# Five blocks of an expert table turned by the vector engine instead of TensorE, in a Trainium2 decoder layer

## The chip, the cores and the metric

The kernel runs on one core of one Trainium2 chip. The core has a matrix engine (TensorE, PE in the profile, with its weight loads as PEld), a vector engine (DVE), a scalar engine (ACT), GpSimd (POOL), a sync engine that only issues transfers (SP), and 16 DMA engines between DRAM and the on-chip memory, which all queues share. The metric is the device time of one execution in microseconds. Before the change it is 943.9 us, the median of three runs from 941.56 to 944.66 us.

## The reference: what is computed

A decoder layer over 256 tokens of width 1024, in float32. A mixer (retention beside block-sparse attention, gated, with an output projection) ends in a residual add. Then, in `peer`, each token takes part in a product-key retrieval of single-neuron experts:

```python
u = u_tab[ec]                                        # rows of peer_u, 16384 x 1024
a = jax.nn.gelu(jnp.einsum('td,thkd->thk', hc, u), approximate=False)
return jnp.einsum('thk,thkd->td', gc * a, v_tab[ec]) # rows of peer_v, 16384 x 1024
```

Each of 8 heads picks 16 experts of 16384 for a token. `ec` holds their numbers and `gc` the softmaxed gates.

## The kernel before, in words

The kernel has three stages on PE's time axis. From 0 to about 302 us it computes the mixer and the queries from weights that stream in. In the second stage, 302 to 649 us, for 176 of the 256 tokens it doesn't gather experts but multiplies with the whole table: `peer_u` is cut into 128 chunks of 128 experts, and for each chunk `c` eight matmuls (L1288) contract the 1024 columns against the transposed activations. The result passes GELU and is multiplied with a dense matrix of gates, `W`, which is built meanwhile from one-hot products (L1160 and L1161 on DVE, L1215 and L1216 on PE). In the third stage, 649 us to the end, the 128 chunks of `peer_v` are multiplied with `W` (L1320, L1321): a chunk V0, V1, ... of v is split into a rounded high part on ACT (L147) and a remainder on DVE (L148), and every tenth pair of chunks is used unsplit (L1318). The tokens that remain have their rows of u and v gathered by GpSimd (L1037) and reduced on DVE (L1048 for u, L1123 for v), woven into the same two stages.

A matmul contracts over partitions, so a chunk of u, loaded with one expert per partition, has to be turned first. Three kinds of chunk differ in who turns them.

- A plain chunk is loaded by one DMA of 512 KB in rows of 4 KB (L682), turned by eight PE transposes into two PSUM banks (L737), and copied out by two ACT instructions (L738) to a tile `rhi`. This is done two iterations ahead of its matmuls, and the matmuls use the activations in the layout `hTf`.
- Every seventh chunk up to number 125 was turned during the mixer: four DMAs of 128 KB, each with 32 partitions and 1 KB runs, brought its quarters to their places (`load_quarters`, L747), DVE turned 32x32 blocks (`turn`, L751), and the result went to a DRAM scratch, `turned`. In the second stage it is loaded from there (L705) and used in place. Its matmuls use the layout `hTd`.
- A chunk listed in the tuple `TURN` is loaded by `load_quarters` on SP's queue and turned by `turn` in the second stage. Before the change the tuple is empty, so there is none.

What sets the order: the instructions of each engine run in the order in which the program writes them. Loads of u and v go through a ring of six slots of 512 KB (`raw_ring`), in order, on SP's queue; a load waits for its slot, which is free when the PE transposes (plain chunk), the DVE turn (chunk of `TURN`), the matmuls themselves (every seventh chunk), or the DVE remainder (a chunk of v) have read it. Each load also takes one of eight completion semaphores in turn and waits for the load that had that semaphore before. The gathers go on GpSimd's own queue, paced by the loop over chunks.

Of the kernel before, what the change touches and what calls it, by code (L numbers as in the profile page):

```python
# [53 lines left out]
STEP = 7  # L54
PRE0 = 14
PERIOD = 3
TURN = ()
WARM = 8
GROW = 96
SK = 16  # L60
# [15 lines left out]
def layer_kernel(ctx, tc, x, mix_norm_g, w_in, ret_w_branch, moba_q_gain, moba_k_gain, moba_w_branch,  # L76
# [26 lines left out]
    def raw_tile(n=1):  # L103

        i = raw_count[0] % RAWS
        raw_count[0] += n
        assert i + n <= RAWS
        return raw_ring[:, i] if n == 1 else raw_ring[:, i:i + n]
# [580 lines left out]
    def load_any(i):  # L689
# [9 lines left out]
        elif i < len(pieces) + NK:  # L699
# [3 lines left out]
            if early_chunk(c):  # L703
                u_raw[c] = raw_tile()
                nc.sync.dma_start(u_raw[c], turned[c // STEP])  # L705
            elif c in TURN:
                u_raw[c] = raw_tile()
# [14 lines left out]
    def transpose_u(c):  # L722

        if c < NK and early_chunk(c):
            u_T[c] = u_raw.pop(c)
        elif c in TURN:
            r = u_raw.pop(c)
# [12 lines left out]
    def early_chunk(c):  # L740
        return c % STEP == STEP - 1 and c // STEP < NPRE
# [530 lines left out]
    for c in range(NK):  # L1272
# [11 lines left out]
        uT = u_T.pop(c)  # L1284
        hT = hTd if c in TURN or early_chunk(c) else hTf
        for k in range(KC):
# [154 lines left out]
```

## Time and profile before

| | |
|---|---|
| median of three runs | 943.9 us (941.56 to 944.66) |
| the profiled execution | 942.91 us, span on the core 941.1 us |
| PE busy | 932.6 us, 99% |
| DVE busy | 794.2 us, 84% |
| ACT busy | 521.1 us, 55% |
| POOL busy | 395.0 us, 42% |
| moved by DMA | 322.50 MB, mean 343 GB/s |

All times inside the execution are microseconds from the start of the span. The median of the runs is 1.0 us above the profiled execution, and that lies 1.8 us above its own span. PE, PEld, DVE, ACT and POOL are told apart by the busy time of each. [...] q1 is the queue of loads that SP issues, q0 that of GpSimd's gathers and q10 ACT's.

### The profile page before, as it was taken

The numbers are of one execution on the slowest core, as the hardware profiler recorded it, in microseconds if no ns is written. First come the engines' busy times: TensorE is split into PE (matmuls) and PEld (weight loads), VectorE is DVE, ScalarE is ACT, GpSimd is POOL, SyncE is SP. The second block draws the span as 40 slices with busy tenths as digits, with TensorE's granted clock in tenths as the row PEclk, the third lists the DMA queues.
The fourth block names the chain that finished last, engine by engine and source line by source line (L and its number), as shares of the span: only waits on it lengthen the run. The fifth ranks groups of instructions, "written<-read, shape, count | busy, mean of one in ns | idle before, by whom it ended". The sixth has DMA issues, their size and how long they took to land.

```text
span 941.1 us, 19115 instructions
## 1 busy us (share of the span) xinstructions
PE 932.6 (99%) x7192; PEld 894.4 (95%) x7192; DVE 794.2 (84%) x1518; ACT 521.1 (55%) x953; POOL 395.0 (42%) x305
## 2 busy tenths in 40 slices
PE   8999999999999999999999999999999999999998
PEld 6887898998999999999999999999999999999997
DVE  6658557788678999999998999974979989898977
ACT  6554655544644435444687778776454645454553
POOL 3412010000202447534656667763547556464720
PEclk9999999999999999999999999999999999999999
DMA  9899879998799997999999999999999999999993
GB/s 317 236 236 283 241 207 292 306 295 264 244 354 386 406 400 285 402 402 361 375 401 390 382 364 381 380 377 367 370 363 398 409 383 409 383 409 374 409 344 125
DMA packets 110858, 322.50 MB, mean 343 GB/s; under 512 B 11532, under 2 KB 23701, under 8 KB 110638
## 3 DMA queue, kind: packets, MB, share of 16 engines
q1 hardware_dynamic: 64492, 184.43, 55.0%
q0 software_dynamic: 32512, 115.54, 32.5%
q10 hardware_dynamic: 13762, 21.31, 7.6%
q8 instruction: 57, 0.93, 0.4%
q14 instruction: 35, 0.29, 0.1%
HBM read 308.57 MB, written 14.19 MB: 343 GB/s over the span
## 4 chain that ended last, share of the span: by engine, by line
PE 95%; DMA 2%; DVE 1%; ACT 0%; POOL 0%; issue 0%; SPq 0%; DVEq 0%; ACTq 0%; POOLq 0%
PE acc L1288 24%; PE side L737 11%; PE side L1320 9%; PE acc L1320 9%; PE acc L230 6%; PE acc L231 6%; PE acc L232 6%; PE acc L1321 4%; PE side L1321 4%; PE acc L239 3%; PE acc L240 3%; PE acc L241 3%; DMA raw_ring<-in_peer_v_dram 2%; PE side L1318 1%; PE acc L1318 1%; PE acc L1216 1%
## 5 line engine op out<-in xcount | busy, mean ns | idle before, releaser
L1037 POOL DMA_INDIRECT rows<-in_peer_u_dram,eg x86 | 110.5, 1285 | 68.4 <-DVE rows L1048 30.2
L1037 POOL DMA_INDIRECT rows<-in_peer_v_dram,eg x54 | 96.0, 1777 | 73.2 <-DVE vacc L1123 51.2
L737 PE MATMUL side<-ident,raw_ring 128*128 128x128 f32 x768 | 103.0, 277 | 0.0
L737 PEld LDWEIGHTS side<-ident,raw_ring 128*128 128x128 f32 x768 | 93.0, 192 | 0.0
L1165 ACT ACTIVATE oh_buf<-oh_more,tS 128x128 bf16<-128x128 f16 x176 | 58.4, 417 | 0.5 <-DVE oh_more L1160 0.5
L1123 DVE SCALAR_TENSOR_TENSOR vacc<-rows,av,vacc 128x1024 f32<-128x1024 f32 x43 | 55.1, 1282 | 0.1
L1048 DVE SCALAR_TENSOR_TENSOR rows<-rows,h 128x1024 f32<-128x1024 f32 x43 | 53.2, 1249 | 1.4 <-DMA rows<-in_peer_u_dram,eg 1.4
L1260 ACT ACTIVATE cw<-W 128x352 fp32r<-128x352 f32 x58 | 28.7, 495 | 45.3 <-PE acc L1321 43.9
L1261 DVE TENSOR_TENSOR cw<-W,cw 128x352 fp32r<-128x352 f32 x58 | 30.2, 521 | 19.8 <-ACT cw L1260 19.6
L1246 POOL TENSOR_TENSOR W<-W,gl 128x256 f32<-128x256 f32 (+19 forms) x31 | 26.4, 850 | 41.9 <-ACT gl L1245 34.0
L580 POOL DMA_DIRECT2D x1d<-xt x1 | 0.7, 657 | 88.5 <-DVE xt L562 88.5
L1288 PE MATMUL acc<-hTd,raw_ring 128*128 128x128 f32 x288 | 35.1, 276 | 0.0
L1160 DVE TENSOR_TENSOR oh_more<-iota,tI 128x1024 f16<-128x1024 f16 x44 | 34.3, 780 | 0.0
L1161 DVE TENSOR_TENSOR oh_buf<-oh_more,tM 128x1024 f16<-128x1024 f16 x44 | 32.3, 734 | 2.2
L1288 PEld LDWEIGHTS acc<-hTd,raw_ring 128*128 128x128 f32 x288 | 33.6, 192 | 0.0
L154 POOL TENSOR_TENSOR gny<-va,minus_half 128x8 f32<-128x8 f32 x2 | 4.3, 2126 | 67.8 <-DVE va L454 67.8
L1215 PE MATMUL acc<-oh_buf 128*128 128x128 bf16 x176 | 24.4, 220 | 0.0
L1216 PE MATMUL acc<-oh_buf 128*128 128x128 bf16 x176 | 24.4, 219 | 0.0
L1229 ACT ACTIVATE W<-acc 128x512 f32<-128x512 f32 (+20 forms) x44 | 17.2, 391 | 12.0 <-PE acc L1216 10.6
L1248 ACT ACTIVATE W<-acc 128x256 f32<-128x256 f32 (+19 forms) x52 | 18.5, 356 | 4.4 <-PE acc L1288 4.4
L1231 DVE TENSOR_TENSOR W<-acc,W 128x264 f32<-128x264 f32 (+19 forms) x32 | 16.2, 507 | 4.7 <-ACT W L1229 4.5
L1215 PEld LDWEIGHTS <-oh_buf 128*128 128x128 f16 x176 | 19.8, 114 | 0.0
(2695 smaller groups left out, 3484.4 us busy)
## 6 DMA issues: line engine op xcount, KB each, us to landing
raw_ring<-in_peer_v_dram SPq DMA_DIRECT2D x128, 512.0 KB, 8.2
raw_ring<-in_peer_u_dram SPq DMA_DIRECT2D x96, 512.0 KB, 9.9
raw_ring<-in_w_in_dram SPq DMA_DIRECT2D x52, 512.0 KB, 5.5
raw_ring<-turned SPq DMA_DIRECT2D x18, 512.0 KB, 7.1
raw_ring<-in_peer_w_q_dram SPq DMA_DIRECT2D x16, 512.0 KB, 6.1
W<-in_peer_u_dram SPq DMA_DIRECT2D x14, 512.0 KB, 11.0
eraw<-in_peer_u_dram ACTq DMA_DIRECT2D x36, 128.0 KB, 6.5
h<-in_peer_u_dram ACTq DMA_DIRECT2D x36, 128.0 KB, 6.6
```

The lines of the kernel that those rows point to most:

```text
L230: T.matmul(o[t], xh[:, s], wh, start=(k == 0), stop=False)
L231: T.matmul(o[t], xh[:, s], wl, start=False, stop=False)
L232: T.matmul(o[t], xl[:, s], wh, start=False, stop=(k == kc - 1))
L737: T.transpose(p[:, k * P:(k + 1) * P], r.rearrange("p (i k) -> p k i", k=KC)[:, 4 * q + k], ident)
L1037: G.indirect_dma_start(out=r, out_offset=None, in_=tab, in_offset=bass.IndirectOffsetOnAxis(ap=eg[:, j:j + 1], axis=0))
L1048: V.scalar_tensor_tensor(r, r, 1.0, h, op0=OP.mult, op1=OP.mult, accum_out=av[:, j:j + 1])
L1123: V.scalar_tensor_tensor(a, r, av[:, j:j + 1], a, op0=OP.mult, op1=OP.add)
L1165: A.activation(o1[:, j], hot[:, 0, :, j], AF.Copy, scale=tS[:, t, k + j:k + j + 1])
L1215: T.matmul(p[:, j * P:(j + 1) * P], hi, o1, start=True, stop=False)
L1288: T.matmul(pa[:, n:n + NA], uT[:, k * P:(k + 1) * P], hT[:, k], start=(c % 2 == 0 and k == 0), stop=(k == KC - 1), skip_group_check=True)
L1320: T.matmul(o[b][:, :2 * ND], vh[:, n], w, start=(c == 0), stop=False, skip_group_check=True)
L1321: T.matmul(o[b][:, :ND], vl[:, n], w[:, :ND], start=False, stop=(c == NK - 1), skip_group_check=True)
```

## The change

The tuple `TURN` names five chunks; nothing else is edited.

```diff
--- before.py
+++ after.py
@@ -54,7 +54,7 @@
 STEP = 7
 PRE0 = 14
 PERIOD = 3
-TURN = ()
+TURN = (122, 123, 124, 126, 127)
 WARM = 8
 GROW = 96
 SK = 16
```

Chunk 125 is one of those turned during the mixer, so from 122 on no chunk is left to PE. The code that now runs for the five chunks was there before:

```python
def load_quarters(queue, dst, c):                                  # L744
    src = peer_u[0, c * P:(c + 1) * P, :].rearrange("(b a) (g d) -> g a b d", a=32, g=4)
    for g in range(4):
        queue.dma_start(dst[32 * g:32 * g + 32].rearrange("a (b d) -> a b d", b=4), src[g])

def turn(dst, src, k):                                             # L749
    V.transpose(dst.rearrange("p (k b a) -> p b k a", k=KC, b=4)[:, :, k],
                src.rearrange("p (b k i) -> p b k i", b=4, k=KC)[:, :, k])

elif c in TURN:                                                    # in transpose_u, L726
    r = u_raw.pop(c)
    u_T[c] = hi_tile(F32)
    for k in range(0, KC, 4):
        turn(u_T[c], r, slice(k, k + 4))
```

Three places show what moves. First PE, at the end of the second stage, after its last one-hot products. The rows are the matmuls of the chunks up to 127 (`x8` is a chunk) and the first of the third stage (L1320). Before:

```order
L737 MATMUL side<-ident,raw_ring 128x128 x8
L1288 MATMUL acc<-hTf,rhi__7278 128x128 x8
L1288 MATMUL acc<-hTf,rhi__7313 128x128 x8
L737 MATMUL side<-ident,raw_ring 128x128 x8
L1288 MATMUL acc<-hTf,rhi__7347 128x128 x8
L737 MATMUL side<-ident,raw_ring 128x128 x8
L1288 MATMUL acc<-hTd,raw_ring 128x128 x8
L1288 MATMUL acc<-hTf,rhi__7382 128x128 x8
L1288 MATMUL acc<-hTf,rhi__7409 128x128 x8
L1320 MATMUL side<-cw,rhi__7433 128x352
```

Now, from chunk 122 (`rhi__7287`) to 127 (`rhi__7384`), chunk 125 being the one that is read from `raw_ring`:

```order
L1288 MATMUL acc<-hTd,rhi__7287 128x128 x8
L1288 MATMUL acc<-hTd,rhi__7315 128x128 x8
L1288 MATMUL acc<-hTd,rhi__7342 128x128 x8
L1288 MATMUL acc<-hTd,raw_ring 128x128 x8
L1288 MATMUL acc<-hTd,rhi__7367 128x128 x8
L1288 MATMUL acc<-hTd,rhi__7384 128x128 x8
L1320 MATMUL side<-cw,rhi__7398 128x352
```

The three groups of transposes here are gone, as are two more ahead of them, and the matmuls of six chunks stand one behind the other. Second DVE at the same place, where the last row products of the gathers (L1048) and the first work on v (L1261, L148) stand:

```order
 L1048 SCALAR_TENSOR_TENSOR rows__7077,av<-rows__7077,h_75 128x1024
+L751 STREAM_TRANSPOSE rhi__7287<-raw_ring 128x4x4x32 x2
 L1048 SCALAR_TENSOR_TENSOR rows__7118,av<-rows__7118,h_75 128x1024
 L1048 SCALAR_TENSOR_TENSOR rows,av<-rows,h_75 128x1024 x2
 L1109 TENSOR_TENSOR av<-av,gg 128x64
```

```order
L751 STREAM_TRANSPOSE rhi__7315<-raw_ring 128x4x4x32 x2
L751 STREAM_TRANSPOSE rhi__7342<-raw_ring 128x4x4x32 x2
L751 STREAM_TRANSPOSE rhi__7367<-raw_ring 128x4x4x32 x2
L751 STREAM_TRANSPOSE rhi__7384<-raw_ring 128x4x4x32 x2
L1261 TENSOR_TENSOR cw<-W,cw 128x2x176
```

The second piece follows the first directly. The turn of chunk 122 stands ahead of the last three row products, the other four behind them and ahead of the first work on v. Third SP's queue, the loads around the border of u and v, each with what it waits for: a `DMAHW` is one of the eight completion semaphores, PE, DVE the engine that frees the slot. Now, from chunk 125 (L705) over 126 and 127 to V0, V1 and V2:

```order
L705 DMA raw_ring_71<-turned_88 128x1024 [waits DMAHW7_49]
L747 DMA raw_ring_71<-in_peer_u_dram 32x4x256 [waits DMAHW0_49]
L747 DMA raw_ring_71<-in_peer_u_dram 32x4x256 [waits DMAHW1_49]
L747 DMA raw_ring_71<-in_peer_u_dram 32x4x256 [waits DMAHW2_49]
L747 DMA raw_ring_71<-in_peer_u_dram 32x4x256 [waits DMAHW3_49]
L747 DMA raw_ring_71<-in_peer_u_dram 32x4x256 [waits DMAHW4_49,PE_49]
L747 DMA raw_ring_71<-in_peer_u_dram 32x4x256 [waits DMAHW5_49]
L747 DMA raw_ring_71<-in_peer_u_dram 32x4x256 [waits DMAHW6_49]
L747 DMA raw_ring_71<-in_peer_u_dram 32x4x256 [waits DMAHW7_49]
L682 DMA raw_ring_71<-in_peer_v_dram 128x1024 [waits DMAHW0_49,DVE_49]
L682 DMA raw_ring_71<-in_peer_v_dram 128x1024 [waits DMAHW1_49,DVE_49]
L682 DMA raw_ring_71<-in_peer_v_dram 128x1024 [waits DMAHW2_49,DVE_49]
```

Before, this stretch was one load of `turned`, two of u and then those of v. A load that needed one place in the row of eight semaphores now needs four, so the last quarter of chunk 127 waits for the landing of chunk 125, and V0 for that of the first quarter of chunk 126.

## The prediction

> **What bounds the kernel now.** I read the page's busy shares, then the chain of waits, then the windows around the border between u and v, where all five chunks lie. First the page's row of busy times:
>
> ```profile
> PE 932.6 (99%) x7192; PEld 894.4 (95%) x7192; DVE 794.2 (84%) x1518; ACT 521.1 (55%) x953; POOL 395.0 (42%) x305
> ```
>
> PE is the bound on the whole, so work taken from it counts, as long as what it then needs is there in time. The windows show whether the DMA engines could deliver earlier (columns: window, its length, busy time of PE, PEld, DVE, ACT, POOL, granted clock, DMA share, GB/s):
>
> ```profile
> 626.00:630.00 4.00, 4.00 (x45) 4.00 (x45) 3.90 (x7) 3.50 (x10) 3.55 (x3) 1.00 0.90 330
> 630.00:634.00 4.00, 4.00 (x38) 4.00 (x38) 2.28 (x5) 2.95 (x7) 2.11 (x4) 1.00 0.95 315
> 634.00:644.00 10.00, 10.00 (x95) 10.00 (x95) 0.00 (x0) 4.06 (x10) 3.30 (x4) 1.00 1.02 409
> 645.00:647.30 2.30, 2.30 (x23) 2.30 (x23) 1.60 (x2) 1.90 (x3) 1.19 (x1) 1.00 0.33 93
> ```
>
> They are a second bound, just under the first: 0.90 to 1.02 busy until the first chunks of v have landed, and only then, from 645 to 647.3, nearly idle. So the question is not what PE saves, but whether V0 and V1 can be there that much sooner.
>
> **What is removed.** The chain of waits gives each chunk's eight transposes with the time that they hold PE (start, length, what):
>
> ```profile
> 629.82 0.95 PE side L737 x8
> ...
> 632.55 0.89 PE side L737 x8
> ...
> 635.67 0.95 PE side L737 x8
> 636.62 3.57 PE acc L1288 x32
> 640.20 0.89 PE side L737 x8
> ...
> 642.87 0.89 PE side L737 x8
> ```
>
> These are chunks 122, 123, 124, 126 and 127: 0.95 + 0.89 + 0.95 + 0.89 + 0.89 = 4.57 us of PE's path, the most that the change can give. The ten ACT copies (L738) leave too; they are off the path.
>
> **What is added on DVE.** The turn's price stands in the mixer's rows, its place in the timeline (start, length, engine, line, operation):
>
> ```profile
> L751 DVE STREAM_TRANSPOSE eT<-eraw x18: 697/705/712, 61.8 to 222.3; 128x512 f32<-128x512 f32 x18
> ...
> 631.87 0.09 DVE L1048 DVE_READ_ACCUMULATOR rows<-rows,h 128x1 f32 x1
> 632.28 0.34 DVE L1109 TENSOR_TENSOR av<-av,gg 128x64 f32<-128x64 f32 x1 [0.32 <-ACT av L1108]
> 644.85 0.53 DVE L1261 TENSOR_TENSOR cw<-W,cw 128x352 fp32r<-128x352 f32 x1 [12.23 <-ACT cw L1260]
> 645.79 1.23 DVE L148 TENSOR_TENSOR rlo__7434<-raw_ring,rhi__7433 128x1024 fp32r<-128x1024 f32 x1 [0.42 <-ACT rhi__7433 L147]
> 647.52 1.23 DVE L148 TENSOR_TENSOR rlo__7451<-raw_ring,rhi__7450 128x1024 fp32r<-128x1024 f32 x1 [0.51 <-ACT rhi__7450 L147]
> ```
>
> Two halves of 0.705 are 1.41 us a chunk, 7.05 in all. Four of the five turns, 5.64 us, fall into the 12.23 us in which DVE now waits; that hole is their cover, and without it they would stand before the first work on v. The turn of 122 pushes the last three row products back, so L1109 ends at 632.62 + 1.41 = 634.0 and the turn of 123 at 635.4. PE without its transposes wants 123 at 636.62 - 0.95 - 0.89 - 0.95 + 1.79 = 635.6 (3.57 for two chunks is 1.79 each). That fits with 0.2 us to spare, so DVE costs nothing by itself, unless data come late.
>
> **What is moved: V0 and V1.** PE begins V0 and V1 here, ACT's splits of both stand below, and the load of V0, issued at 630.80, has the time to landing at the end of its row:
>
> ```profile
> 648.87 0.41 PE L1320 MATMUL side<-cw,rhi__7433 128*128 128x352 f32 x1
> 651.10 0.36 PE L1320 MATMUL side<-cw,rhi__7450 128*128 128x352 f32 x1
> ```
>
> ```profile
> 644.70 1.06 ACT L147 ACTIVATE rhi__7433<-raw_ring 128x1024 fp32r<-128x1024 f32 x1
> 646.43 1.06 ACT L147 ACTIVATE rhi__7450<-raw_ring 128x1024 fp32r<-128x1024 f32 x1 [0.40 <-DMA raw_ring<-in_peer_v_dram]
> ```
>
> ```profile
> 630.80 18.31 SPq L682 DMA_DIRECT2D raw_ring<-in_peer_v_dram  x8
> raw_ring<-in_peer_v_dram SPq DMA_DIRECT2D x1, 512.0 KB, 13.1
> ```
>
> V0 lands at 630.80 + 13.1 = 643.9; with 1.06 of ACT and 1.23 of DVE behind that it could be ready at 646.2, 2.6 us before PE takes it. V1 lands at 646.4 (ACT waited for it), is ready at 647.52 + 1.23 = 648.75, and PE takes it at 651.10: 2.35 us of slack. So 2.35 of the 4.57 us can be had at most while the loads land as now. They can hardly land sooner: V0's slot, held by chunk 122, comes free with DVE's turn at about 629.8 instead of 630.8, but 13.1 us of waiting is a queue of transfers, and the same bytes stand ahead.
>
> **What the 1 KB runs cost.** No load in 1 KB runs stands beside gathers of 4 KB rows in this trace. The nearest rows are the mixer's, where the runs go beside the weights' 2 KB rows (121 to 122 and 197.5 to 202.5) or alone (122 to 123, every packet under 2 KB):
>
> ```profile
> 121.00:122.00 1.00, 1.00 (x11) 1.00 (x10) 0.29 (x1) 0.20 (x1) 0.00 (x0) 1.00 1.06 380
> 122.00:123.00 1.00, 1.00 (x12) 1.00 (x10) 0.00 (x0) 0.86 (x1) 0.00 (x0) 1.00 1.14 217
> 197.50:198.50 1.00, 1.00 (x6) 0.84 (x5) 0.35 (x1) 0.62 (x1) 0.00 (x0) 1.00 1.12 355
> 198.50:202.50 4.00, 4.00 (x20) 3.30 (x19) 2.73 (x3) 1.06 (x1) 0.00 (x0) 1.00 1.08 230
> ...
> DMA packets 241, 0.22 MB, mean 217 GB/s; under 512 B 29, under 2 KB 241, under 8 KB 241
> ```
>
> The engines are fully busy in all four and move as little as half of the 409 GB/s of 4 KB rows. A chunk is 0.524 MB: 1.28 us at 409, 1.38 at 380, 2.42 at 217. Over the five us from 197.5 the mean is (355 + 4 x 230)/5 = 255 GB/s, a loss of 5 x (1 - 255/409) = 1.9 us. So a chunk costs 0.1 to 1.9 us of all engines' time more than now; I take 1.13, the lone runs' row, which lies between the ends.
>
> [...]
>
> Five chunks cost 5 x 1.13 = 5.65 us. Of this the gaps take something: 626 to 634 lacks 4 x (79 + 94)/409 = 1.7 us of full rate, or by busy share 0.6 us; I take 1.2. That leaves 4.45 us by which the queue empties later (0 to 8.9 from the ends).
>
> One thing works the other way. While 1 KB runs and other packets share the engines, they take turns packet by packet (145 to 146 us, packets and MB of the two queues):
>
> ```profile
> q1 hardware_dynamic: 93, 0.19, 70.4%
> q10 hardware_dynamic: 84, 0.08, 43.8%
> ```
>
> So gathers of 4 KB rows would go ahead, V0 to V2 would come out last and alone, and V1 would land up to one load, 1.28 us, ahead of the queue's end, where it now lands with it. I take half, 0.6.
>
> **What is late next.** SP's queue holds twenty quarters instead of five loads, and the last quarter of 127 waits for the landing of chunk 125:
>
> ```profile
> 626.61 1.30 SPq L705 DMA_DIRECT2D raw_ring<-turned  x1
> DMA to landing us min/median/max: 8.4/8.4/8.4
> ...
> DMA to landing us min/median/max: 2.6/6.6/11.2
> ```
>
> The first two are chunk 125, which lands at 635.0, the last the mixer's quarters. 635.0 plus 6.6 and a turn of 1.41 is 643.0. PE, 4.57 us ahead, would end 127 at 648.87 - 4.57 = 644.3 and so wants it at 644.3 - 1.79 = 642.5. With three chunks' loss ahead (3 x 1.13 - 1.2 = 2.2) PE stands 2.7 us there, and V0 is behind 127 in SP's queue. This is less than what V1 asks for, so it doesn't add.
>
> **Sum.** V1 is ready 4.45 - 0.6 later, of which 2.35 is slack: the third stage runs 1.5 us later than now. It passes this on, since PE has no idle time there to catch up with (1.07 us in 680 to 700, none else up to 920):
>
> ```profile
> 680.00:700.00 20.00, 18.93 (x138) 18.51 (x137) 15.29 (x17) 9.99 (x12) 7.99 (x5) 1.00 0.95 345
> 700.00:720.00 20.00, 20.00 (x149) 20.00 (x148) 19.96 (x20) 9.53 (x11) 16.81 (x8) 1.00 1.00 389
> 720.00:920.00 200.00, 200.00 (x1454) 199.85 (x1452) 181.07 (x180) 104.00 (x125) 107.55 (x58) 1.00 1.01 391
> ```
>
> The profiled execution took 942.91 us and would take 944.4; the median of the runs is 1.0 above it, so 945.4. A change under 0.3%, 2.8 us, can't be told from none here.
>
> **The rivals.** First, the runs cost nothing, as the row of 380 GB/s suggests for their beginning: then 2.35 us are gained at V1, and up to 1.25 more if v's loads also come out of the queue ahead: 941.5 to 940.3, at the very most 943.9 - 4.57 = 939.3. For it: a share of 0.90 to 0.95 still has gaps. Against it: 217 GB/s at full share. Second, on the other side, the runs hold back everything beside them as from 198.5: 5 x 1.9 - 1.2 = 8.3 us, less 0.6 and 2.35 is 5.3 us late at V1, 949.2. It is slower by over 0.3% from (2.8 + 2.35 + 0.6 + 1.2)/5 = 1.4 us a chunk. For it: most of the mixer's loads ran beside others. Against it: fewer gathers stand beside SP's loads at 628. Third, the semaphores decide: quarters take 11.2 instead of 6.6 us, 127 is turned at 635.0 + 2.2 + 11.2 + 1.41 = 649.8, PE ends it at 651.6, and V0 follows 2.7 us late: 946.6. That the five chunks aren't moved to DVE at all can't be: the instructions are there.
>
> **How the numbers follow.** Forecast (V1 decides, -1.9 to +2.8 us) 0.45; first rival 0.24, of which 0.18 lies beyond 0.3%; second 0.27; third 0.04, half of it on either side of the bound. Faster 0.18, within 0.3% 0.45 + 0.06 + 0.02 = 0.53, slower 0.29. The range from 940.3 to 949.3 reaches from the first rival's gain to the second's loss and leaves some 0.1 on either side.
>
> **What would show it.** Right: PE stands 2 to 6 us between the last u chunks and V1, on ACT and DVE that wait for `raw_ring`; the DMA engines are busy at 230 to 330 GB/s around 628 to 636 us; the gap at 645 to 647.3 is gone; DVE's turns take 0.70 us. Wrong: PE starts V1 before 648.3, the rate stays near 400 GB/s under the runs, or the loss lies elsewhere: in gathers that come late to DVE before 632, or in the third stage.

## The result, and the profile after

The changed kernel takes 950.27 us, the median of six runs (949.11 to 951.66), beside 943.61 us (941.56 to 944.66) for the kernel before in the same comparison: 1.0077 times as long, with an interval from 1.0063 to 1.0090. It is slower, by 6.7 us. The profiled execution has a span of 948.1 us; before it was 941.1, so 7.0 us longer.

The page of the kernel after gives the busy times. PE works 2.4 us less than before and stands longer:

```profile
PE 930.2 (98%) x7152; PEld 891.7 (94%) x7152; DVE 801.4 (85%) x1528; ACT 516.6 (54%) x943; POOL 397.2 (42%) x305
```

Where it stands is read from the windows around the border between u and v (window, its length, busy time of PE, PEld, DVE, ACT, POOL, granted clock, DMA share, GB/s). The DMA share is the mean busy share of the 16 DMA engines; it can pass 1.00, as at 122 to 123 us in the kernel before, where q10 alone had 114.0%. After:

```profile
626.00:630.00 4.00, 4.00 (x43) 4.00 (x42) 3.90 (x6) 3.89 (x11) 3.49 (x3) 1.00 1.02 326
630.00:634.00 4.00, 4.00 (x42) 4.00 (x41) 0.00 (x1) 0.97 (x3) 2.52 (x3) 1.00 1.11 242
634.00:644.00 10.00, 3.22 (x28) 2.90 (x27) 6.25 (x11) 1.02 (x3) 3.35 (x3) 0.77 1.05 269
644.00:648.00 4.00, 4.00 (x28) 4.00 (x28) 1.30 (x2) 0.77 (x2) 0.67 (x1) 0.71 1.06 242
648.00:652.00 4.00, 2.57 (x22) 2.23 (x20) 0.00 (x0) 0.00 (x0) 0.06 (x1) 1.00 0.50 118
652.00:656.00 4.00, 2.75 (x24) 2.72 (x24) 2.93 (x5) 0.63 (x1) 0.00 (x0) 1.00 0.95 306
...
680.00:700.00 20.00, 20.00 (x146) 20.00 (x145) 16.90 (x18) 10.06 (x13) 8.09 (x6) 1.00 1.01 387
```

The windows of the kernel before that the prediction doesn't show:

```profile
644.00:648.00 4.00, 4.00 (x38) 4.00 (x38) 2.23 (x3) 3.09 (x5) 1.50 (x1) 1.00 0.49 159
648.00:652.00 4.00, 4.00 (x33) 4.00 (x33) 1.90 (x2) 2.51 (x4) 1.71 (x2) 1.00 1.01 407
652.00:656.00 4.00, 4.00 (x32) 4.00 (x31) 3.48 (x6) 3.90 (x6) 1.02 (x1) 1.00 1.03 407
```

From 626 to 656 us PE worked all 30 us before, and now 20.54. What strikes is the DMA share beside the rate, the last two columns: the DMA engines are fully busy (1.02 to 1.11) from 626 to 648 and move 242 to 326 GB/s, where 409 went through at 634 to 644 before. They are not short of work; each byte takes them longer. It begins with chunk 122's quarters: at 620 to 626 us 324 GB/s went through at a share of 1.05, before 412 at 1.03. Then, at 648 to 652, they stand half idle, as nothing new has been issued.

PE's waits in the kernel after, from 600 us on (what waited, for what: us in all, times, longest), say for whom it stands:

```profile
PE acc L1288 <- DVE rhi__7315 L751: 6.4, 1, 6.4
PE acc L1288 <- DMA raw_ring<-turned: 1.4, 1, 1.4
PE acc L1288 <- DVE rhi__7367 L751: 1.2, 1, 1.2
PE side L1321 <- DVE rlo__7399 L148: 0.4, 1, 0.4
PE acc L1288 <- DVE rhi__7287 L751: 0.4, 1, 0.4
```

`rhi__7287`, `7315`, `7342`, `7367` and `7384` are the turned chunks 122, 123, 124, 126 and 127. DVE's timeline after shows that it is not DVE that is late (start, length, operation, and in brackets its own wait):

```profile
634.02 1.30 DVE L751 STREAM_TRANSPOSE rhi__7287<-raw_ring 128x512 f32<-128x512 f32 x2 [4.01 <-DMA raw_ring<-in_peer_u_dram]
...
642.56 1.31 DVE L751 STREAM_TRANSPOSE rhi__7315<-raw_ring 128x512 f32<-128x512 f32 x2 [3.28 <-DMA raw_ring<-turned]
645.59 1.30 DVE L751 STREAM_TRANSPOSE rhi__7342<-raw_ring 128x512 f32<-128x512 f32 x2 [1.73 <-DMA raw_ring<-in_peer_u_dram]
652.43 1.31 DVE L751 STREAM_TRANSPOSE rhi__7367<-raw_ring 128x512 f32<-128x512 f32 x2 [5.54 <-DMA raw_ring<-in_peer_u_dram]
654.38 1.30 DVE L751 STREAM_TRANSPOSE rhi__7384<-raw_ring 128x512 f32<-128x512 f32 x2 [0.64 <-DMA raw_ring<-in_peer_u_dram]
```

A turn takes 1.30 us for both halves, and each waits for its load. (At chunk 123 the bracket names the load of chunk 125. By the order of the semaphores its own last quarter is the one to go by: the third quarter of 126 waits for it, and SP issues that at 642.36, just ahead of the turn.) SP's own queue of the kernel after (start, length, what it issues, how many) has the loads:

```profile
613.74 20.49 SPq L747 DMA_DIRECT2D raw_ring<-in_peer_u_dram  x12
636.24 0.34 SPq L705 DMA_DIRECT2D raw_ring<-turned  x1
638.51 11.77 SPq L747 DMA_DIRECT2D raw_ring<-in_peer_u_dram  x8
651.25 4.79 SPq L682 DMA_DIRECT2D raw_ring<-in_peer_v_dram  x6
```

Chunk 122's first quarter is issued at 613.74 and its turn can begin at 634.02, 20 us later. From the ninth on each quarter waits for the one that had its semaphore before, so SP needs 20.49 us to issue twelve quarters, and V0 is issued at 651.25, which was 630.80 before.

Last, PE's timeline after:

```profile
634.88 2.02 PE L1288 MATMUL acc<-hTd,rhi__7287 128*128 128x128 f32 x16 [0.36 <-DVE rhi__7287 L751]
643.32 3.45 PE L1288 MATMUL acc<-hTd,rhi__7315 128*128 128x128 f32 x16 [6.42 <-DVE rhi__7315 L751]
...
656.95 0.41 PE L1320 MATMUL side<-cw,rhi__7398 128*128 128x352 f32 x1
```

V0's first product comes at 656.95, 8.1 us later than at 648.87. The matmuls of chunk 123, behind the stand of 6.42 us, have a row of 3.45 us where that of a chunk is otherwise 1.95 us long, and the granted clock of their windows is 0.77 and 0.71. The account: waits of 9.5 us ahead of V0, plus 1.5 for the slow clock (3.45 less 1.95), less the 4.57 us of transposes, is 6.4; V0 is 1.7 later than that, of which 0.6 lies ahead of the first chunk of u, and the rest is not taken apart. The end is 7.0 later, since the 1.07 us that PE stood idle at 680 to 700 are gone.

### The profile page after: what moved, and what is told of

It is laid out like the page before. It is cut to its first block, busy times and chain, and to the rows that moved or that the text cites. A ratio compares the mean times of both kernels' runs of the same rounds, so it can differ in the third digit from the quotient of the medians.

```text
span 948.1 us, 19074 instructions
## 1 busy us (share of the span) xinstructions
PE 930.2 (98%) x7152; PEld 891.7 (94%) x7152; DVE 801.4 (85%) x1528; ACT 516.6 (54%) x943; POOL 397.2 (42%) x305
## 4 chain that ended last, share of the span: by engine, by line
PE 93%; DMA 5%; DVE 1%; ACT 0%; POOL 0%; issue 0%; SPq 0%; DVEq 0%; POOLq 0%
PE acc L1288 22%; PE side L737 10%; PE acc L1320 9%; PE side L1320 9%; PE acc L230 6%; PE acc L231 6%; PE acc L232 6%; PE side L1321 4%; PE acc L1321 4%; PE acc L239 3%; PE acc L240 3%; PE acc L241 3%; DMA raw_ring<-in_peer_u_dram 2%; PE side L1318 2%; PE acc L1318 2%; DMA raw_ring<-turned 1%
## 5 line engine op out<-in xcount | busy, mean ns | idle before, releaser
L1037 POOL DMA_INDIRECT rows<-in_peer_v_dram,eg x54 | 98.7, 1828 | 72.3 <-DVE vacc L1123 57.8
L737 PE MATMUL side<-ident,raw_ring 128*128 128x128 f32 x728 | 97.6, 277 | 0.0
L737 PEld LDWEIGHTS side<-ident,raw_ring 128*128 128x128 f32 x728 | 88.2, 192 | 0.0
L1048 DVE SCALAR_TENSOR_TENSOR rows<-rows,h 128x1024 f32<-128x1024 f32 x43 | 53.0, 1247 | 2.0 <-DMA rows<-in_peer_u_dram,eg 2.0
L1261 DVE TENSOR_TENSOR cw<-W,cw 128x352 fp32r<-128x352 f32 x58 | 30.1, 519 | 13.6 <-ACT cw L1260 12.9
```

Source lines behind the costliest of these rows:

```text
L737: T.transpose(p[:, k * P:(k + 1) * P], r.rearrange("p (i k) -> p k i", k=KC)[:, 4 * q + k], ident)
L1037: G.indirect_dma_start(out=r, out_offset=None, in_=tab, in_offset=bass.IndirectOffsetOnAxis(ap=eg[:, j:j + 1], axis=0))
L1048: V.scalar_tensor_tensor(r, r, 1.0, h, op0=OP.mult, op1=OP.mult, accum_out=av[:, j:j + 1])
```

## The experiments

The question is why loads that move the same bytes take the engines half as long again (269 GB/s at full share, where 409 went through before). Four properties came with the change: DVE turns, runs of 1 KB instead of 4, four loads a chunk instead of one, and 32 neighbouring partitions a load instead of 128. The first four kernels take them apart. Several kernels put rows where the turn doesn't want them; their numbers come out mixed up, and nothing is left out of the work. In the diffs the line that is replaced is the call of `load_quarters` in `load_any`.

**wide_4k: the turn alone.** One load of 4 KB rows a chunk. The work on every engine is that of the change.

```
 TURN = (122, 123, 124, 126, 127)
-                load_quarters(nc.sync, u_raw[c], c)
+                nc.sync.dma_start(u_raw[c], peer_u[0, c * P:(c + 1) * P, :])
```

> The five chunks are turned on DVE as in the change, but each comes in one load of 512 KB with 4 KB rows over 128 partitions, as before the change; the experts and columns of the five chunks are therefore mixed up, and only the time counts. If the 1 KB quarters are the cause of the loss, by whatever mechanism (sharing, number of loads or partition span), it is gone: V0's first matmul comes at 645.5 to 647 instead of 648.9 (before) and 657.0 (changed), bounded by the landing of V0 and V1, and the time is 1.9 to 2.8 us below before, about 941.3. If the turns on DVE (their place ahead of row products and of the first work on v) are the cause, the loss stays: 947 or more.

938.42 us, 0.9966 times the time before (0.9953 to 0.9978). The turn on DVE gains, and more than the prediction's bound: 3.8 us against 2.35. The whole loss lies in the loads.

**quarters_pe: the loads alone.** The quarters are loaded as in the change, and TensorE turns the chunks as before.

```
-        elif c in TURN:
-            ...
-        hT = hTd if c in TURN or early_chunk(c) else hTf
+        hT = hTd if early_chunk(c) else hTf
```

> The loads of the change (quarters in 1 KB runs), but TensorE turns the chunks as before, so DVE has no added work; the data of the five chunks are mixed up. If the loads alone are the cause, the time is that of the change plus about what PE's transposes would have saved where PE isn't waiting: 950 to 954, V0 at 657 or later. If DVE's turns in DVE's order make the loss, it is gone: 943 to 945.

952.17 us, 1.0107 (1.0084 to 1.0129): with the loads of the change and nothing of its gain, it is as slow as the change or slower; the two intervals just overlap.

**one_1k: the runs alone.** One load a chunk over 128 partitions, each partition in four runs of 1 KB, whose starts overlap.

```
+                nc.sync.dma_start(u_raw[c].rearrange("p (b d) -> p b d", b=4),
+                                  bass.AP(tensor=peer_u.tensor, offset=peer_u.offset + c * P * D, ap=[[D, P], [240, 4], [1, 256]]))
```

> As the change, but a chunk comes in one load over 128 partitions in four runs of 1 KB each (the runs overlap in the source, so the data of the five chunks are wrong). Run length of the change, without its four loads and without the span of 32 partitions. Sharing theory: chunk 122 still lands after 628 and SP's queue still moves 60 to 100 KB per us beside gathers, so PE still stands some us at the end of the second stage: 946 to 950. Number of loads, or partition span: no loss, 941 to 943.5.

939.35 us, 0.9972 (0.9960 to 0.9985), 0.0006 above wide_4k, 0.6 us, which is within the intervals. The length of the runs, on which the prediction put its price, costs next to nothing by itself.

**four_4k: number and place.** Four loads of 32 whole rows each, of 4 KB.

```
+                for g in range(4):
+                    nc.sync.dma_start(u_raw[c][32 * g:32 * g + 32], peer_u[0, c * P + 32 * g:c * P + 32 * g + 32, :])
```

> As the change, but a chunk's four loads take 32 rows of 4 KB each instead of 32 partitions x 4 runs of 1 KB, so the number of loads, the semaphores they take and the span of 32 partitions are those of the change and only the run length differs; the data of the five chunks are mixed up. Sharing theory (1 KB packets take turns one for one with the gathers' 4 KB packets and get a fifth of the bytes): the loss is gone, 941 to 943.5, V0 before 649. Number of loads and semaphores: a load waits for the landing of the eighth before it whatever its run length, so V0 waits as in the change: 947 to 951. Partition span (32 partitions take about half the rate): half of the loss, 944 to 947.

946.78 us, 1.0043 (1.0026 to 1.0059): 0.0077 above wide_4k, 7.3 us of the 10.5 that the change has above it (1.0077 against 0.9966). The window of 634 to 644 us, in which loads of u still run, in each kernel, first wide_4k, then one_1k, four_4k and quarters_pe:

```profile
634.00:644.00 10.00, 10.00 (x93) 9.81 (x91) 6.92 (x13) 3.11 (x7) 4.15 (x6) 1.00 1.02 410
```

```profile
634.00:644.00 10.00, 9.99 (x93) 9.80 (x92) 6.62 (x14) 1.78 (x5) 4.48 (x5) 1.00 1.05 394
```

```profile
634.00:644.00 10.00, 6.22 (x47) 6.03 (x46) 5.18 (x11) 1.14 (x4) 2.60 (x3) 0.83 1.03 302
```

```profile
634.00:644.00 10.00, 5.57 (x35) 5.41 (x36) 1.46 (x3) 1.94 (x4) 2.78 (x3) 0.81 1.04 308
```

At equal DMA share, the loads over 128 partitions go with 394 to 410 GB/s and those over 32 with 302 to 308 (269 in the changed kernel). Two causes were left: theory A, the number of loads (eight semaphores, so eight quarters in flight at most), and theory B, the 32 partitions.

**cols_4: number without the place.** Four loads a chunk of 1 KB runs, as many and as large as in the change, but each over all 128 partitions (each takes its quarter of the columns).

```
+                for g in range(4):
+                    nc.sync.dma_start(u_raw[c][:, 256 * g:256 * (g + 1)], peer_u[0, c * P:(c + 1) * P, 256 * g:256 * (g + 1)])
```

> The five chunks again by four loads each and turned by the vector engine, but each load takes 1 KB of each of the 128 rows: four loads a chunk as in the changed kernel, runs of 1 KB as there, but each load spans all 128 partitions. (A piece is put at its own place in the row, not where the turn wants it: the numbers come out mixed up.) Theory A, the number of loads: as the changed kernel (950.3) or four_4k (946.8), 945 to 951 us. Theory B, the span of 32 partitions: as one_1k (939.4), 938 to 942 us.

940.09 us, 0.9969 (0.9954 to 0.9984). Twenty loads of 1 KB runs with the same order of semaphores, and it is as fast as with five; SP stands 5.8 us on earlier quarters there, in the changed kernel 21.2, so those waits follow from the slow loads. That leaves the partitions: cols_4 and the change differ in nothing else about the loads but in which partition each run goes to. The queues' rows show what this does to others. In 634 to 646 us the gathers' queue (q0: packets, MB, share of 16 engines' time), in the kernel before, in the changed one and in cols_4:

```profile
q0 software_dynamic: 587, 2.12, 44.1%
```

```profile
q0 software_dynamic: 563, 2.04, 65.1%
q1 hardware_dynamic: 883, 1.17, 39.8%
```

```profile
q0 software_dynamic: 535, 1.93, 41.1%
```

The share times 16 engines and 12 us, over the MB, is the engines' time for a MB: 39.9 us before, 61.3 in the changed kernel, 40.9 in cols_4; for a row of 4 KB 0.164, 0.251 and 0.168 us. The gathers are the same in all three, and nothing about them was edited. So the loads into 32 neighbouring partitions didn't only take long themselves, they held up what the gathers' queue moved beside them (61.3 us a MB against 40.9 in cols_4).

**rows_125: number without the place, in another way.** Four loads of 125, 1, 1 and 1 rows.

```
+                for lo, hi in ((0, 125), (125, 126), (126, 127), (127, 128)):
+                    nc.sync.dma_start(u_raw[c][lo:hi], peer_u[0, c * P + lo:c * P + hi, :])
```

> As four_4k (chunks 122, 123, 124, 126 and 127 loaded in whole rows of 4 KB by four loads each, and turned by the vector engine; the rows are not put where the turn wants them, so the numbers come out mixed up), but the four loads take 125, 1, 1 and 1 rows. So there are as many loads as in four_4k, 20 for the five chunks, and nearly every byte comes in a load that spans 125 partitions. Theory A, the number: SyncE's queue lets a load go only when the load eight before it has landed, so that four loads a chunk hold two chunks in flight at most, and that is what costs: about as four_4k (946.8), 944 to 949 us. Theory B, the span: a load that spans 32 partitions is slow and slows the gathers beside it, wherever it stands: as wide_4k (938.4), 937 to 941 us. Between the two (941 to 944) both have a share.

963.39 us, 1.0215 (1.0193 to 1.0236), which neither theory had. Two of its windows, in which little else was moved:

```profile
644.00:648.00 4.00, 1.78 (x9) 1.49 (x7) 0.00 (x0) 0.77 (x2) 0.72 (x1) 0.50 0.33 127
652.00:656.00 4.00, 4.00 (x20) 4.00 (x20) 0.17 (x1) 0.00 (x0) 0.00 (x0) 0.50 0.33 132
```

The share is 0.33, a third of the 1.02 that went with 409 GB/s, and the rate, 130 GB/s from 646 to 656 us, a third of 409. So the engines were mostly idle while a load of 125 rows was under way; why isn't shown. That is a loss of another kind than the low rate at full share, and the run doesn't count for either theory.

**turn_126_127: two chunks of the change.** `TURN = (126, 127)`.

> The change for chunks 126 and 127 alone: 8 of its 20 quarter loads, 2 of the 5 chunks taken from TensorE (0.89 us each). If the loss goes by the number of quarter loads, whichever way they cost: the loads of all five cost 950.3 - 938.4 = 11.9 us and the turns save 943.6 - 938.4 = 5.2 us, so two fifths of both, 4.8 - 2.1: 2.7 us slower, 945 to 947 us. Theory A, the number of loads in flight: only the eight loads of these two chunks and the one of 125 wait for an earlier quarter, and V0's and V1's behind them, so it costs less than its share: 941 to 945 us. Theory B, the span: two fifths, 945 to 947 us.

946.74 us, 1.0027 (1.0005 to 1.0050). It is slower than the kernel before, and it fits two fifths of the loss (0.4 x 0.0077 is 0.0031); the interval is too wide to say more.

**Which partitions.** Theory B now has two forms: B1, the place that a load writes to, and B2, the few rows of a load. Three kernels put them to the test.

half_64, two loads of 64 rows of 4 KB:

```
+                for g in range(2):
+                    nc.sync.dma_start(u_raw[c][64 * g:64 * g + 64], peer_u[0, c * P + 64 * g:c * P + 64 * g + 64, :])
```

> As four_4k, but each of the five chunks in two loads of 64 neighbouring partitions (0 to 63, 64 to 127). Theory B1 in its plain form, the share of the partitions that a load reaches: half of the loss of four_4k against wide_4k (946.8 - 938.4 = 8.4 us) or less, 939 to 943 us. Theory B2, few rows in a load: half of it or less too, 939 to 943 us. [...]

949.27 us, 1.0077 (1.0053 to 1.0102). Twice as many partitions a load gained nothing. Both forms as they stood there, with half of the loss or less, fell. That half_64 is, if anything, slower than four_4k (1.0043) isn't explained.

mid_64, where the 64 rows of one load lie across the middle:

```
+                for lo, hi in ((32, 96), (0, 32), (96, 128)):
+                    nc.sync.dma_start(u_raw[c][lo:hi], peer_u[0, c * P + lo:c * P + hi, :])
```

> As half_64 (five chunks in whole rows of 4 KB, turned by the vector engine, data mixed up), but the loads take partitions 32 to 95, 0 to 31 and 96 to 127. So half of the bytes again come in a load of 64 neighbouring partitions, which lies across the middle and not in one half. [...] Theory B2, that loads of 64 or fewer rows are slow wherever they stand: as half_64 or, with more loads, above it, 948 to 952 us.

945.53 us, 1.0030 (1.0016 to 1.0045). More loads than half_64, and two of them of 32 rows, and still faster: about two fifths of the way from half_64 to wide_4k by the ratios. So it counts where the 64 rows lie, and the 948 to 952 us of theory B2 did not come. The windows, half_64 first:

```profile
634.00:644.00 10.00, 1.82 (x17) 1.63 (x16) 4.65 (x9) 1.02 (x3) 2.02 (x3) 0.85 1.04 296
```

```profile
634.00:644.00 10.00, 7.93 (x60) 7.75 (x59) 4.06 (x9) 1.78 (x5) 5.10 (x5) 0.83 1.04 311
```

stride_4, 32 rows a load on every fourth partition:

```
+                for g in range(4):
+                    nc.sync.dma_start(u_raw[c][g:P:4], peer_u[0, c * P + 32 * g:c * P + 32 * g + 32, :])
```

> As four_4k (five chunks in four loads of 32 whole rows each, turned by the vector engine, data mixed up), but the 32 rows of a load go to every fourth partition (g, g+4, g+8, ...) and not to 32 neighbours. The number of loads, the rows and bytes of each, the run length and the source are the same. [...] Theory B2, the size: a load of 32 rows gives each engine two packets only, and that is what is slow: as four_4k (946.8), 945 to 949 us. [...]

953.00 us, 1.0115 (1.0093 to 1.0138). Theory B1 would have the time of wide_4k here (938.42), so this looks like theory B2. But the edit did something else as well: the framework that orders the instructions seems to treat a strided piece as if it overlapped other slots: TensorE's transposes of three plain chunks now wait for the strided loads (the order of PE's instructions, four_4k with -, stride_4 with +):

```
-L738 MATMUL side<-ident,raw_ring 128x128 [waits DMAHW0_49,PE_49]
+L738 MATMUL side<-ident,raw_ring 128x128 [waits DMAHW4_49,DMAHW5_49,DMAHW3_49,DMAHW6_49,DMAHW0_49,PE_49]
```

PE's waits in stride_4, 600 to 660 us, show the price, which four_4k does not have:

```profile
PE side L738 <- DMA raw_ring<-in_peer_u_dram: 10.6, 3, 5.0
```

So its time tells nothing between the theories. Its queues do: from 618 to 626 us strided loads and gathers run side by side, as quarters and gathers do in four_4k; stride_4 first, then four_4k:

```profile
q0 software_dynamic: 678, 2.46, 77.8%
```

```profile
q0 software_dynamic: 345, 1.28, 61.2%
```

The whole moves 399 GB/s in the first and 266 in the second. The gathers' MB takes 0.778 x 16 x 8 / 2.46 = 40.5 us beside the strided loads and 61.2 beside the loads into neighbours. Loads of 32 rows didn't hold up the gathers when they were spread; it is the place.

**order_0213: the quarters in another order.** The changed kernel with `for g in (0, 2, 1, 3)` in `load_quarters`.

> The changed kernel with the four quarter loads of a chunk issued in the order 0, 2, 1, 3 (in the early turns of the first stage as well): the result is the same. A load can still run beside the one that was issued just before it. [...] Theory B1 in its plain form, and B2: as the changed kernel, 949 to 952 us.

948.52 us, 1.0056 (1.0036 to 1.0075). The interval overlaps the change's (1.0063 to 1.0090), so it decides nothing.

**placed: the whole change, loads over 128 partitions.** The five chunks are copied from memory to memory during the first stage, in the order of the quarters, and loaded from there by one load each.

```
+    placed = dr.tile([len(TURN), P, D], F32, name="placed")
...
-                load_quarters(nc.sync, u_raw[c], c)
+                nc.sync.dma_start(u_raw[c], placed[TURN.index(c)])
...
+        if step == 1 and m % 3 == 2 and 0 <= m < 3 * len(TURN):
+            load_quarters(nc.scalar, placed[m // 3], TURN[m // 3])
```

> The whole change with other loads, the result being the same: during the first stage ScalarE's queue copies the five chunks from memory to memory in the order of the quarters (1 KB runs), and in the second stage SyncE loads each chunk from that copy by one load of 128 rows of 4 KB; the vector engine turns it as in the changed kernel. If only the loads' way into the partitions costs (theory B1), the second stage goes as in wide_4k, 938.4 us, plus what the 20 copies cost in the first stage: they move 2.6 MB, 9 to 11 us of the transfers' time at the 236 to 300 GB/s of that stage, beside a TensorE that is 99% busy there; 0 to 3 us of it may show: 938 to 942 us. If the turns on the vector engine, or anything else that wide_4k's mixed up data left out, had a part: 943 us and more.

949.19 us, 1.0069 (1.0052 to 1.0086), not the 938 to 942 expected. The loss lies in the first stage: ACT issues the copies, and its work stands behind them until they are issued (8.17 us below). The timeline of ACT and PE's longest wait in placed:

```profile
206.35 4.63 ACTq L748 DMA_DIRECT2D placed<-in_peer_u_dram  x4
211.08 1.06 ACT L147 ACTIVATE rhi__1954<-raw_ring 128x1024 fp32r<-128x1024 f32 x1 [8.17 <-DMA placed<-in_peer_u_dram]
```

```profile
PE side L542 <- DVE sa L536: 5.6, 2, 5.4
```

The first product of u came 10.7 us later than before, while u itself took 4.4 us less.

**placed_pool: the same copies from GpSimd's queue**, which has little to do there.

```
-        if step == 1 and m % 3 == 2 and 0 <= m < 3 * len(TURN):
-            load_quarters(nc.scalar, placed[m // 3], TURN[m // 3])
+        if step == 1 and m % 2 == 0 and 0 <= m < 2 * len(TURN):
+            load_quarters(nc.gpsimd, placed[m // 2], TURN[m // 2])
```

> As placed, but the 20 copies are issued by GpSimd's queue, and somewhat earlier in the first stage, where GpSimd has little to do (2.6 us of work in 100 to 140 us, 1.6 us in 140 to 180 us of the kernel before). In placed, from the first product of u to the first of V it took 341.9 us (before 346.3, wide_4k 342.2), but the first product of u came at 313.3 us and not at 302.6: ScalarE stood behind its own copies (8.2 us at 206 us) and TensorE behind it. If the place that a load reaches is the whole cause of the loss, and the copies' bytes are hidden, u starts within 1 us of 302.6 us again and the time is that of wide_4k, 938 to 940.5 us. If the bytes of the copies themselves hold up the weights of the first stage, u starts at 305 us and later, and the time is 941 us and more. If the loads from the copy cost more than plain rows, u to V takes 345 us and more.

938.75 us (937.54 to 939.87), 0.9957 times the time before (0.9941 to 0.9973): faster than both kernels, and the time of wide_4k. Its windows and V0's first product:

```profile
630.00:634.00 4.00, 4.00 (x42) 4.00 (x41) 4.00 (x7) 1.06 (x3) 2.56 (x3) 1.00 0.98 364
634.00:644.00 10.00, 10.00 (x96) 10.00 (x94) 6.20 (x12) 2.69 (x6) 3.62 (x5) 1.00 1.02 404
...
680.00:700.00 20.00, 20.00 (x149) 20.00 (x148) 18.66 (x20) 12.32 (x15) 12.18 (x6) 1.00 1.03 408
```

```profile
645.13 0.41 PE L1323 MATMUL side<-cw,rhi__7404 128*128 128x352 f32 x1
```

PE doesn't stand, 404 GB/s go through, and V starts 3.7 us earlier than before. u starts at 303.28 us (302.57 before), so the copies are hidden. The turns and the result are those of the change, and with other loads its loss of 6.7 us is a gain of 3.7. Place, number and run length of the loads are changed here together; cols_4, which keeps the number and the runs and is as fast, says that it is the place.

## Why the prediction was wrong, step by step

**PE saves 4.57 us: right.** Without trouble from the loads, placed_pool runs u in 4.4 us less (wide_4k 4.1) and gains 3.7 at the end (wide_4k 3.8).

**DVE costs nothing by itself: right.** In wide_4k and placed_pool PE never waits for a turn; the 12.23 us hole took them. A turn takes 1.30 us, where 1.41 was reckoned.

**Only 2.35 us can be had, since loads land as now: wrong.** V0 starts 3.7 us earlier in placed_pool. The loads can land sooner, although V0's own is issued no earlier (630.65 against 630.80): from 626 to 634 the engines carry 383 and 364 GB/s, before 330 and 315, and ACT's split of V1, which waits for its load, starts at 645.65 instead of 646.43. After its third load of v SP waits for a slot until 641.83, before until 645.57, so the gap of 644 to 648 is filled (412 GB/s against 159), and the idle 1.07 us at 680 to 700 goes too.

**The price of the 1 KB runs: this is the step that failed.** The prediction took the half rate of the lone quarters (217 GB/s) for the price of short runs, 1.13 us a chunk (0.1 to 1.9). one_1k and cols_4 put runs of 1 KB at 0.6 and 0.3 us for all five chunks, neither clear of noise. The rate was low because of the other property of the same loads, the 32 partitions, and that property costs more beside gathers, since it slows them too. By rate: wide_4k moves 4 x 377 + 4 x 341 + 10 x 410 + 4 x 409 = 8.61 MB from 626 to 648 us, the changed kernel 5.93; the 2.68 MB that lack are 6.5 us at 409 GB/s. From 614 to 626 another 6 x (412 - 390) + 6 x (409 - 324) is 0.64 MB, 1.6 us, and the half idle window behind them is another 2.6. That is 10.7 us, 2.1 a chunk, or 1.6 without the idle window, where the prediction had 1.13. With 2.1, and without the 0.6 of the next step, its own sum gives 5 x 2.1 - 1.2 - 2.35, about 7 us late, near the 6.7 measured; that is in part luck, since the 2.35 is wrong too. The second rival's price (1.9) lies between, and its time, 949.2, is within 1.1 us of the result. It had the size from the right row, the mixed 230 GB/s, and the cause wrong as well: what holds back the others is not the runs.

The error of reasoning was to take the price from the row of the lone loads (217 GB/s), in which what they do to others can't be seen. That the packets of both queues take longer beside loads into neighbouring partitions is shown (in four_4k, by the rows below, 56.1 us a MB for the gathers, where 39.9 were taken before, and 54.7 for the loads), and that it goes by the place; what in the chip holds them up isn't shown. The mixed row had the effect on others in it. These are the weights' rows on q1 in the kernel before, at 121 to 122 us, where the whole moved 380 GB/s, and at 198.5 to 202.5, where it moved 230:

```profile
q1 hardware_dynamic: 103, 0.18, 46.6%
```

```profile
q1 hardware_dynamic: 286, 0.56, 58.3%
```

The share times 16 engines and 1 or 4 us, over the MB, is 41 and 67 us of the engines a MB. It was the row to go by.

**Turns packet by packet: the gain of 0.6 us did not come.** In the queues' rows of 634 to 646 us the loads of the changed kernel got 1.17 MB through beside 2.04 MB of gathers, in four_4k (4 KB rows, same places) 1.61 beside 1.97:

```profile
q0 software_dynamic: 536, 1.97, 57.6%
q1 hardware_dynamic: 538, 1.61, 45.9%
```

The shorter packets do get less, but those that were held back stand ahead of V0 in SP's queue, so that it is late, not early. Most of the 3.2 us between four_4k and the changed kernel (1.0043 and 1.0077) may be this; no run takes it apart.

**What is late next: too small, and not the last of it.** A stand of 2.7 us at chunk 127 was forecast, which was not to add. PE stood 9.8 us in all, 9.5 of them ahead of V0, and most of it at 123, for 6.4 us: the quarters of 122 had all landed 20 us after the first was issued, where 6.6 were reckoned, and those of 123 behind them. What the step missed is that the stands come before V0 in the same queue, so that V0 is issued 20 us late. The semaphores alone, the third rival, are not it: cols_4 has as many loads and waits and loses nothing.

**The third stage passes the shift on: nearly.** It gave 1.07 us back; the idle time at 680 to 700 is gone in the changed kernel and in placed_pool, so that it belonged to the moment at which V started and not to the stage.

**What would show it.** PE standing on loads (9.5 us, not 2 to 6), rates of 230 to 330 GB/s around 628 to 636, and turns of 0.70 us a half were seen; the gap at 645 to 647.3 was filled, and a new one opened at 648 to 652. These signs could not tell the forecast's cause from the real one, since both give a low rate at full share.

## What to carry to other kernels

When a row shows a low rate at full DMA share, list every property in which those transfers differ from the fast ones (run length, loads a block, partitions) before giving one of them the price: here kernels with one property changed showed that it was the partitions. Load over all 128 partitions where other queues run (391 to 410 GB/s here, against 269 to 311 with loads into 32 or 64 neighbours), and if the data must be put in another order, do it where the engines have time, from a queue on which nobody waits. A slow transfer's price includes what it does to the transfers of other queues (61.3 us a MB of gathers against 39.9) and to what stands behind it in its own (V0 issued at 651.25 instead of 630.80).

## What was not expected of the hardware

- Loads into 32 neighbouring partitions slowed the transfers of another queue: a gathered row of 4 KB took 0.251 us of an engine beside the quarters and 0.164 without. From 634 to 644 us the whole moved 269 to 311 GB/s at full share with loads into 32 or 64 neighbours, against 391 to 410 with loads over all 128.
- Where the partitions lie counted here, and twice as many of them gained nothing: loads into 64 neighbours of one half (949.27 us) were no better than into 32 (946.78), with half of the bytes across the middle it was faster than half_64 (945.53), and beside loads into every fourth partition the gathers took 40.5 us a MB where they took 61.2 beside loads into 32 neighbours.
- While a load of 125 rows ran with little beside it, the DMA share was 0.33 and the rate 130 GB/s.
- PE paid twice for a stand. After 6.42 us the row of a chunk's sixteen matmuls was 3.45 us long, after 8.18 us (half_64) 3.79, and 1.95 otherwise; the granted clock was 0.77 and 0.71 in the windows of the first and 0.52 in that of the second, from 644 to 648 us. In rows_125, with stands of 4.0 to 5.9 us, it was 0.50 in both windows. In mid_64 the row behind a stand of 2.06 us was 3.64 long (granted clock 0.83 from 634 to 644 us), while behind stands of 1.43 and 1.25 us in the changed kernel the rows were 2.05 and 2.02 long. At what length of a stand the clock falls isn't shown. PE's row in mid_64:

```profile
638.72 3.64 PE L1289 MATMUL acc<-hTd,rhi__7311 128*128 128x128 f32 x16 [2.06 <-DVE rhi__7311 L752]
```
